# A planner that keeps accounts of every engine's queue, paired attention heads, and a reordered RWKV preparation in a hybrid encoder trunk

## The chip, the cores and the metric

The kernel runs on one core of one Trainium2 chip. The metric is the device time of one execution in microseconds (us), as the median of several runs.

## The reference

Two token groups, a prompt of 512 tokens and a sample of 256, pass through the same two layers with shared weights (model width 1024). A layer is a SwiGLU feed-forward half step, a mixer, and a second feed-forward half step, each behind an RMS norm that is scaled, shifted and gated by vectors made from a condition (`w_ada`). The mixer projects its input to 2432 columns (19 tiles of 128) and runs three head groups on them: a bidirectional gated linear recurrence (LRU), a bidirectional RWKV-7 with 4 heads of 64, and attention with 6 query heads on 2 key heads.

```python
def attention(q, k, v, q_g, k_g, rope):
    ...
        sc = jnp.einsum("bqkgd,bskd->bkgqs", qi, k) * scale
        p = jax.nn.softmax(sc, axis=-1)
        return jnp.einsum("bkgqs,bskd->bqkgd", p, v)
...
def layer(x, c, lp, rope):
    ...
    x = x + 0.5 * g1 * swiglu(h, lp["ffn_w_in"][0], lp["ffn_w_out"][0])
    h = rmsnorm(x, lp["norm_g"][1]) * (1 + sc2) + sh2
    x = x + g2 * mixer(h, lp, rope)
    h = rmsnorm(x, lp["norm_g"][2]) * (1 + sc3) + sh3
    x = x + 0.5 * g3 * swiglu(h, lp["ffn_w_in"][1], lp["ffn_w_out"][1])
```

## The kernel before

Activations lie transposed, 128 features on the partitions and the tokens along a row. The kernel calls the prompt `PS` (512 tokens, q.i = 0) and the sample `SS` (256 tokens, q.i = 1).

**Dense work.** Every product with a large weight (`mm3`) is made of three fp32r matmuls per 128x128 block: high part by high part, high by low, low by high. `wload` (lines 268 to 272) makes a weight's two parts: ScalarE copies the raw tile to `wh`, VectorE subtracts it to get `wl`, both inside `tc.high_priority(offset=60)`, which lets them stand up to 60 instructions ahead of their place in the program. Seven tiles of each part are held (`NW`). On TensorE the dense products go by the names of what they write: `pg`, `pu` (feed-forward input, prompt), `pb` (the same, sample), `mip` (mixer input), `ops` (output projections). A matmul of 512 columns is the prompt's, of 256 the sample's.

**Other work.** `adaps` makes the condition vectors, `ssp` the norms' sums. In `attention`, a unit is one head of one block of 128 queries: `S` (scores, a contraction of 64 rows), a softmax on VectorE and ScalarE, `ptp` (four or two transposes of the probabilities) and `avp` (values, 64 output rows). The two heads of a pair, hh = 0 and 1, lie on the lower and the upper 64 partitions. `gps` are the LRU's gates. In `rwkv_pair` (two heads at a time) a preparation makes decay (`up`, scanned into `cu`), rate (`ap`, `aa`), the normed key (`kkp`, `kb`) and the bonus (`bp`), and from them `AR`, `BK` and a copy `B`; then come `scps`, the block inverse (`yps` and `dps`, four levels), and a chain over the chunks of 64 tokens, `zps`, `saps`, `stps`, each waiting for the one before by way of VectorE or ScalarE; at the end `ywp`, a group norm and `yp`.

**What sets the order.** TensorE's order is written by the program itself (`tc.manual_schedule` for that engine); the other engines follow the program's order by priority, as a scheduler places it. The program's order comes from a planner (`Sched`): each sequence has a dense thread, and attention, LRU, RWKV and the condition vectors are threads beside them. Every matmul moves the planner's clock on by a cost; a thread that yields a number is ready that much later; a ready thread that isn't dense goes first. The numbers are fixed in a table `LAT`, one per kind of step and sequence:

```python
LAT = {'R0': (1.0, 4.4), 'ACC': (7.4, 2.8), ...
    def step(self, th):
        ...
        if callable(r):
            th.cond = r
        else:
            th.ready = self.t + r
```

Of the kernel before, what the change touches and what calls it, by code (L numbers as in the profile page):

```python
# [15 lines left out]
KD = 8  # L16
# [35 lines left out]
NR = 4  # L52

# [7 lines left out]
class Sched:  # L61
# [9 lines left out]
    def step(self, th):  # L71
        try:
            r = next(th.gen)
        except StopIteration:
            th.done = True
            self.threads.remove(th)
            return
        th.cond = None
        if callable(r):
            th.cond = r  # L80
        else:
            th.ready = self.t + r

    def run(self):
        while self.threads:
            act = [th for th in self.threads if th.cond is None or th.cond()]
            assert act, "stuck"
            now = [th for th in act if th.ready <= self.t + 1e-9]
            if not now:
                self.t = min(th.ready for th in act)  # L90
                continue
# [6 lines left out]
            else:  # L98
                self.step(dn[0])
                self.debt = max(0.0, self.debt - (self.t - t0))  # L100

# [10 lines left out]
def trunk_kernel(ctx, tc, xT, cT, wadh, wada, wfi, wfo, wmi, wmo, prm, gatew, loraw, cst, rope, scanm, outT, dbg=None):  # L112
    nc = tc.nc
    V, A, G, PE = nc.vector, nc.scalar, nc.gpsimd, nc.tensor
    sch = Sched(RATIO)

# [4 lines left out]
    sm = ctx.enter_context(tc.tile_pool(name="small", bufs=5))  # L121
# [8 lines left out]
    def dbank(n=512, name="db"):  # L130
        return psd.tile([128, n], F32, name=name, tag="d")

    def sbank(n=512, name="sb"):
        return pss.tile([128, n], F32, name=name, tag="m")
# [11 lines left out]

    def mm(out, lhsT, rhs, start=True, stop=True, cost=None):
        PE.matmul(out, lhsT, rhs, start=start, stop=stop, skip_group_check=True)  # L148
        k, m, n = lhsT.shape[0], lhsT.shape[-1], rhs.shape[-1]
        if cost is not None:  # L150
            sch.t += cost
        elif rhs.dtype == F32R:
            sch.t += (n / 2.4 if n >= 256 else 213) * 1e-3
        else:
            conc = 1.0
            if m <= 32:
                conc = 4.0
            elif m <= 64:
                conc = 2.0
            sch.t += max(4 * max(n, m) / 2.4 / conc, 33.0) * 1e-3  # L160

    def trp(out, src, idn, cost=0.11):
        PE.transpose(out, src, idn)
        sch.t += cost
# [47 lines left out]
    def ada_load(src):  # L212
        u = adap.tile([128, 1024], F32, name="adaw", tag="adaw")
        nc.sync.dma_start(out=u, in_=src)
# [22 lines left out]
    def ada(l, m, lat):  # L237
        ps = sbank(256, name="adaps")
        for k in range(KD):
            for j, u in enumerate(ada_load(wada[l * 9 + m, k])):  # L240
                mm(ps[32 * j:32 * j + 32, :], sc[:, k, :], u, start=(k == 0), stop=(k == KD - 1))
            if k % ADQ == ADQ - 1:
                yield lat
# [20 lines left out]
    def wtile(dt, name):  # L264
        return wsp.tile([128, 512], dt, name=name, tag=name)
# [30 lines left out]
    def weight_raw(u):  # L296
        raw = wsp.tile([128, 1024], F32, name="wr", tag="wr", bufs=NR)
        nc.sync.dma_start(out=raw[:, :u.shape[-1]], in_=u)
# [40 lines left out]
    def mm3(out, q, xs, every):  # L339
        nk = len(xs)  # L340
        for k, (xh, xl) in enumerate(xs):
            if k % 4 == 0:
                wh, wl = wget(q)
            c = (k % 4) * 128
            for i, (a, b) in enumerate(((wh, xh), (wh, xl), (wl, xh))):
                mm(out, a[:, c:c + 128], b, start=(k == 0 and i == 0), stop=(k == nk - 1 and i == 2))
            if k % every == every - 1:
                yield 0.0
# [36 lines left out]
    class Norm:  # L385
# [19 lines left out]
        def apply(self):  # L405
            q, l, i = self.q, self.l, self.i
            self.x = []
            for k in range(KD):
# [11 lines left out]
                yield LAT["CH"][q.i] if k < KD - 1 else LAT["NRM"][q.i]  # L420

        def finish(self):
            yield LAT["ACC"][self.q.i]
# [96 lines left out]
    def mix_in(q, l, xs, M):  # L520
# [3 lines left out]
        nc.sync.dma_start(out=rp, in_=rope[:, :, 0:n])  # L524
# [70 lines left out]
    def attention(q, l, M):  # L595
        n, nt = q.n, q.nt
        yield lambda: M.stage >= 1
        yield LAT["A0"][q.i]
# [22 lines left out]
        yield LAT["A1"][q.i]  # L621
        units = [(j, qt, hh) for j in range(3) for qt in range(nt) for hh in range(2)]
        st = {}

        def stA(u):
            j, qt, hh = units[u]
            b0, c0 = 64 * hh, qt * 128
            S = sbank(n, name="S")
            mm(S, M.qs[j][b0:b0 + 64, c0:c0 + 128], kr[b0:b0 + 64, :])
            mx = tn(1, name="mx")  # L630
            V.tensor_reduce(out=mx, in_=S, axis=AX.X, op=ALU.max)
            c = (j * nt + qt) * 2 + hh
            nb = tn(1, name="nb")
            V.scalar_tensor_tensor(out=nb, in0=mx, scalar=-1.0, in1=rq[:, c:c + 1], op0=ALU.mult, op1=ALU.mult)
            Pm = small(n, name="P")
            ssum = tn(1, name="ssum")
# [642 lines left out]
```

## Time and profile before

| | |
|---|---|
| runs | 3457.16, 3459.14, 3462.76 us; median 3459.14 |
| the profiled execution | 3462.16 us, span 3459.2 us |
| TensorE matmul busy | 3341.5 us, 97% of the span |
| VectorE, ScalarE, GpSimd busy | 58%, 42%, 15% |
| mean granted TensorE clock | 0.986 |

In the rows further down, a matmul's time is from its start to its modelled end, and matmuls overlap, so what one costs is the distance from its start to the next one's. One fp32 matmul stands as two records. The number in brackets is idle time of the engine before the row, and what ended it.

### The profile page before, as it was taken

To read this page: it belongs to the slowest core of one execution; us is meant where nothing else is said; L and a number is where in the kernel's file an instruction comes from. 1 tells how busy PE (TensorE), PEld (TensorE's weight loads), DVE (VectorE), ACT (ScalarE), POOL (GpSimd) and SP (SyncE) were. 2 spreads that over 40 slices of the span, in tenths; PEclk is the share of its full clock that TensorE was granted. 3 is DMA by queue.
4 is the path that set the end of the run, shared out by engine and by line. 5 is a ranking of instruction groups with operands and counts; after the bars stand their busy time and mean duration, and the time that the engine had idled before them with its cause. 6 is when DMAs were issued, how large, how long until landed. Compare 5 with 4: busy or idle time off the path is not lost. (4 is left out here: it accounts for less than half of the span.)

```text
span 3459.2 us, 69173 instructions
## 1 busy us (share of the span) xinstructions
PE 3341.5 (97%) x28052; PEld 2734.0 (79%) x28052; DVE 2003.2 (58%) x3973; ACT 1448.2 (42%) x2730; POOL 512.1 (15%) x659
## 2 busy tenths in 40 slices
PE   7999999999899899999999999999899999999999
PEld 5777776678877777888888876788789978778899
DVE  4433365775776745546333476667557776446466
ACT  3322243644346433434333346534345564334354
POOL 1100020212221211111000111212211111111010
PEclk9999999999999999999999999999899999999999
DMA  7666674133342222423332331233245533223455
GB/s 276 219 206 208 203 270 145 57 104 113 100 153 93 83 80 83 132 90 119 92 98 86 119 114 62 79 110 102 82 161 164 179 106 108 63 91 125 138 177 161
DMA packets 151630, 445.80 MB, mean 129 GB/s; under 512 B 16912, under 2 KB 20752, under 8 KB 151312
## 3 DMA queue, kind: packets, MB, share of 16 engines
q1 hardware_dynamic: 151312, 441.39, 40.2%
q8 instruction: 220, 3.60, 0.4%
q14 instruction: 98, 0.80, 0.1%
HBM read 427.17 MB, written 14.16 MB: 128 GB/s over the span
## 5 line engine op out<-in xcount | busy, mean ns | idle before, releaser
L270 ACT ACTIVATE wh<-wr 128x512 fp32r<-128x512 f32 (+1 forms) x1368 | 816.6, 602 | 1572.1 <-PE ops L148 485.5
L271 DVE TENSOR_TENSOR wl<-wr,wh 128x512 fp32r<-128x512 f32 (+1 forms) x1368 | 907.3, 668 | 800.4 <-ACT wh L270 769.8
L148 PE MATMUL ops<-an,wh 128*128 128x512 f32 (+1 forms) x2816 | 717.8, 345 | 19.3 <-ACT an L351 7.3
L148 PEld LDWEIGHTS ops<-an,wh 128*128 128x128 f32 x2816 | 480.1, 190 | 99.1 <-issue 13.5
L148 PE MATMUL pb<-xn,wh 128*128 128x256 f32 x2816 | 525.1, 287 | 0.5 <-issue 0.5
L148 PE MATMUL ops<-an,wl 128*128 128x512 f32 (+1 forms) x1408 | 477.2, 339 | 0.1
L148 PE MATMUL pg<-xn,wh 128*128 128x512 f32 x1408 | 449.5, 400 | 7.8 <-ACT xn L417 5.9
L148 PEld LDWEIGHTS pb<-xn,wh 128*128 128x128 f32 x2816 | 433.6, 189 | 19.2 <-issue 11.2
L148 PE MATMUL pu<-xn,wh 128*128 128x512 f32 x1408 | 447.4, 399 | 0.0
L352 POOL TENSOR_TENSOR an<-sg,an 128x512 fp32r<-128x512 f32 (+1 forms) x176 | 192.3, 1093 | 1674.0 <-ACT an L351 1613.0
L148 PE MATMUL pb<-xn,wl 128*128 128x256 f32 x1408 | 396.4, 282 | 4.8 <-DVE wl L271 3.8
L431 DVE SCALAR_TENSOR_TENSOR x<-ops,gat,x 128x256 f32<-128x256 f32 (+1 forms) x352 | 215.8, 614 | 196.0 <-PE ops L148 190.6
L148 PE MATMUL mip<-xn,wh 128*128 128x512 f32 (+1 forms) x1216 | 314.2, 348 | 9.3 <-DVE f L583 2.9
L148 PEld LDWEIGHTS pg<-xn,wh 128*128 128x128 f32 x1408 | 260.1, 188 | 75.6 <-ACT xn L417 6.5
L148 PEld LDWEIGHTS pu<-xn,wh 128*128 128x128 f32 x1408 | 260.1, 188 | 65.5 <-issue 6.6
L148 PEld LDWEIGHTS ops<-an,wl 128*128 128x128 f32 x1408 | 267.0, 190 | 31.6 <-DVE wl L271 0.3
L148 PE MATMUL pg<-xn,wl 128*128 128x512 f32 x704 | 277.4, 394 | 0.0
L148 PE MATMUL pu<-xn,wl 128*128 128x512 f32 x704 | 276.8, 393 | 0.0
L148 PEld LDWEIGHTS pb<-xn,wl 128*128 128x128 f32 x1408 | 265.9, 189 | 6.0 <-DVE wl L271 4.8
L148 PEld LDWEIGHTS mip<-xn,wh 128*128 128x128 f32 x1216 | 208.2, 192 | 48.9 <-issue 12.3
L148 PE MATMUL mip<-xn,wl 128*128 128x512 f32 (+1 forms) x608 | 207.2, 341 | 0.0
L148 PEld LDWEIGHTS pg<-xn,wl 128*128 128x128 f32 x704 | 132.9, 189 | 30.7
(257 smaller groups left out, 3738.5 us busy)
## 6 DMA issues: line engine op xcount, KB each, us to landing
wr<-in_wfi_dram SPq DMA_DIRECT2D x352, 512.0 KB, 3.6
adaw<-in_wada_dram SPq DMA_DIRECT2D x128, 512.0 KB, 4.4
wr<-in_wfo_dram SPq DMA_DIRECT2D x192, 256.0 KB, 2.7
wr<-in_wfo_dram SPq DMA_DIRECT2D x128, 320.0 KB, 2.9
wr<-in_wmi_dram SPq DMA_DIRECT2D x76, 512.0 KB, 3.6
wr<-in_wmo_dram SPq DMA_DIRECT2D x32, 512.0 KB, 3.5
adaw<-in_wadh_dram SPq DMA_DIRECT2D x32, 256.0 KB, 5.2
xsp<-x SPq DMA_DIRECT2D x8, 512.0 KB, 3.6
```

The source lines that it names most:

```text
L148: PE.matmul(out, lhsT, rhs, start=start, stop=stop, skip_group_check=True)
L270: A.activation(out=hi[:, :n], in_=raw, func=AF.Copy)
L271: V.tensor_tensor(out=lo[:, :n], in0=raw, in1=hi[:, :n].bitcast(F32), op=ALU.subtract)
L352: eng.tensor_tensor(out=lo, in0=src, in1=hi.bitcast(F32), op=ALU.subtract)
L431: V.scalar_tensor_tensor(out=q.x[m], in0=ps, scalar=gat[l][:, i, m, q.i:q.i + 1], in1=q.x[m], op0=ALU.mult, op1=ALU.add)
```

## The change

The planner's clock stays, but the fixed numbers go where a step's result is known. `Engine` wraps VectorE, ScalarE and GpSimd and enters each instruction in an account (`Model`): how long it takes, when its inputs are written, when its bank is free. A thread now yields `At(time)`, the time at which the account says that its data are there; a matmul whose data are late moves the planner's clock to that time; a thread that needs several PSUM banks asks for them (`mo.banks`). Matmul costs are raised a little, and a change between dense and other work costs 0.1. The pool `small` has 7 buffers in place of 5.

Attention takes both heads of a pair as one unit, in three steps (`scores`, `turn`, `values`), with the two heads' matmuls next to each other. RWKV's preparation makes key norm and bonus first, takes the rate and its product with the key into `BK` early, and ends with `AR`; one addition goes from GpSimd to VectorE. The group norm at the end of a pair (`tail`) is a thread of its own, so the second pair may begin before it. `wload` loses its precedence.

```diff
@@ class Sched
+        elif isinstance(r, At):
+            th.ready = r.t
+        elif r > 0 and self.mo.step_last > 0:
+            th.ready = self.mo.step_last + 0.05
...
+class Model:
...
+    def mm(self, out, ins, cost, old):
+        t = self.sch.t
+        need = max(self.ready(*ins), self.free.get(self.keys(out)[0][0], 0.0))
+        if need > t + 0.02:
...
+            t = need
+        dense = ins[1].dtype == F32R
+        if dense != self.dense:
+            t += SWITCH
...
     def wload(raw, n):
         hi, lo = wtile(F32R, "wh"), wtile(F32R, "wl")
-        with tc.high_priority(offset=60):
-            A.activation(out=hi[:, :n], in_=raw, func=AF.Copy)
-            V.tensor_tensor(out=lo[:, :n], in0=raw, in1=hi[:, :n].bitcast(F32), op=ALU.subtract)
+        A.activation(out=hi[:, :n], in_=raw, func=AF.Copy)
+        V.tensor_tensor(out=lo[:, :n], in0=raw, in1=hi[:, :n].bitcast(F32), op=ALU.subtract)
...
-        units = [(j, qt, hh) for j in range(3) for qt in range(nt) for hh in range(2)]
+        units = [(j, qt) for j in range(3) for qt in range(nt)]
...
+            for hh in range(2):
+                b0 = 64 * hh
+                mm(S[hh], M.qs[j][b0:b0 + 64, c0:c0 + 128], kr[b0:b0 + 64, :], cost=n * 1.25e-3)
...
             for kt in range(nt):
-                mm(o[b0:b0 + 64, :], vt[:, kt * 128 + b0:kt * 128 + b0 + 64], PT[:, kt * 128:kt * 128 + 128],
-                   start=(kt == 0), stop=(kt == nt - 1))
...
+                for hh in range(2):
+                    b0 = 64 * hh
+                    mm(o[b0:b0 + 64, :], vt[:, kt * 128 + b0:kt * 128 + b0 + 64], PT[hh][:, kt * 128:kt * 128 + 128],
+                       start=(kt == 0), stop=(kt == nt - 1))
...
             if u < nu:
-                stA(u)
+                yield from mo.banks(2)
+                scores(u)
+                yield At(mo.ready(*(list(st[u - 1]) if u else [kr])))
+            if 1 <= u <= nu:
+                yield from mo.banks(2)
+                turn(u - 1)
...
             if u >= 2:
-                stC(u - 2)
-            if 1 <= u <= nu:
-                stB(u - 1)
-            yield LAT["A2"][q.i]
+                values(u - 2)
+                yield 0.0
...
+        kp, bp = sbank(n, name="kkp"), sbank(n, name="bp")
+        mm(kp, blk, ksq)
+        mm(bp, blk, bon)
+        V.tensor_tensor(out=bon, in0=v, in1=bp, op=ALU.mult)
+        rB = bc_rsqrt(kp, n, None, None, clamp=1e-24)
...
-        G.tensor_scalar(cs_, cs_, 1.0, None, ALU.add)
+        V.tensor_scalar(cs_, cs_, 1.0, None, ALU.add)
...
+            V.tensor_scalar(BK[d][:, :, 64:128], c3(at_[:, d, :]), d_["kah"][:, hp:hp + 1], d_["ka1"][:, hp:hp + 1], ALU.mult, ALU.add)
+            G.tensor_tensor(out=BK[d][:, :, 64:128], in0=BK[d][:, :, 64:128], in1=c3(k), op=ALU.mult)
...
+        M.tails.append(sch.spawn(tail()))
```

The number of instructions on each engine is the same before and after (21,880 matmuls and transposes on TensorE), and so are their shapes, but for small ones in the softmax and in the preparation. The order moves everywhere. Three places follow, each first as before and then as now.

TensorE, the prompt's attention in layer 0 (`S` scores, `avp` values, `ptp` transposes, `mip` and `pb` dense work of the prompt and of the sample), before:

```order
L148 MATMUL S<-qr 128x512
L148 MATMUL avp<-PT,sqz 64x128 x4
L163 MATMUL ptp<-cs,P 128x128 x4
L148 MATMUL mip<-xn,wh 128x512 x2
L148 MATMUL mip<-xn,wl 128x512
L148 MATMUL mip<-xn,wh 128x512 x2
L148 MATMUL mip<-xn,wl 128x512
```

and now:

```order
L315 MATMUL S<-qr 128x512 x2
L315 MATMUL pb<-xn,wh 128x256 x2
L315 MATMUL pb<-xn,wl 128x256
L315 MATMUL pb<-xn,wh 128x256 x2
L315 MATMUL pb<-xn,wl 128x256
L332 MATMUL ptp<-cs,P 128x128 x8
L315 MATMUL pb<-xn,wh 128x256 x2
L315 MATMUL pb<-xn,wl 128x256
L315 MATMUL pb<-xn,wh 128x256 x2
L315 MATMUL pb<-xn,wl 128x256
L315 MATMUL avp<-P,sqz 64x128 x8
```

Two heads' scores, transposes and values now stand together, and each of the three is a visit of its own between dense matmuls.

VectorE, the end of the first RWKV preparation of the prompt (`rB` and `kb` end the key norm, `sg` and `x` belong to the sample's feed-forward), before:

```order
L378 STREAM_TRANSPOSE rB<-y 128x512
L431 SCALAR_TENSOR_TENSOR x_112<-ops,gat_134,x_112 128x256
L763 TENSOR_TENSOR kb<-kb,rB 128x512
L271 TENSOR_TENSOR wl<-wr,wh 128x512 x2
L781 SCALAR_TENSOR_TENSOR AR<-kb,Pt 128x512 x2
L271 TENSOR_TENSOR wl<-wr,wh 128x512 x2
L784 SCALAR_TENSOR_TENSOR csum<-aa,kb 128x1024
L271 TENSOR_TENSOR wl<-wr,wh 128x512 x2
L787 SCALAR_TENSOR_TENSOR BK<-csum,cu 128x8x64 x2
```

and now:

```order
L129 STREAM_TRANSPOSE rB<-y 128x512
L129 TENSOR_TENSOR kb<-kb,rB 128x512
L129 SCALAR_TENSOR_TENSOR sg<-sg,pb 128x256
L129 TENSOR_SCALAR csum<-csum 128x1024
L129 TENSOR_TENSOR sg<-sg,pb 128x256
L129 SCALAR_TENSOR_TENSOR cu<-smk,csum 128x512 x2
L129 TENSOR_SCALAR BK<-aa,kah_4005,ka_0_4003 128x8x64 x2
L129 TENSOR_TENSOR wl<-wr,wh 128x512 x3
L129 SCALAR_TENSOR_TENSOR sg<-sg,pb 128x256
L129 TENSOR_TENSOR wl<-wr,wh 128x512
L129 TENSOR_TENSOR sg<-sg,pb 128x256
L129 SCALAR_TENSOR_TENSOR csum<-aa,kb 128x1024
```

The key norm now stands ahead of the scans that give `cu`, and the weights' low parts (`wl`) still stand between the preparation's instructions.

TensorE, the chain over the chunks in layer 0 where dense work runs out (the prompt's second pair), before:

```order
L148 MATMUL stps<-SAV,BT 64x64 x4
L148 MATMUL zps<-S_10243,AR 64x64 x4
L148 MATMUL saps<-zt,Th 64x64 x4
L148 MATMUL stps<-SAV,BT 64x64 x4
L148 MATMUL zps<-S_10243,AR 64x64 x4
L148 MATMUL ssp<-acc,cs 128x256
L148 MATMUL saps<-zt,Th 64x64 x4
```

and now:

```order
L315 MATMUL zps<-S_10849,AR 64x64 x4
L315 MATMUL saps<-zt,Th 64x64 x4
L315 MATMUL stps<-SAV,BT 64x64 x4
L315 MATMUL zps<-S_10849,AR 64x64 x4
L315 MATMUL saps<-zt,Th 64x64 x4
L315 MATMUL gps<-xc,gw 64x256 x4
L315 MATMUL stps<-SAV,BT 64x64 x4
L315 MATMUL gps<-xc,gw 64x256 x4
L315 MATMUL zps<-S_10849,AR 64x64 x4
L315 MATMUL saps<-zt,Th 64x64 x4
L315 MATMUL stps<-SAV,BT 64x64 x4
L315 MATMUL zps<-S_10849,AR 64x64 x4
```

In both orders some steps of the chain have no dense matmul between them; the stretch is longer now.

## Rows read from the trace of the kernel before

**Rows 1.** The page, part 1: busy time, share of the span and instructions of TensorE

```profile
PE 3341.5 (97%) x28052; PEld 2734.0 (79%) x28052; DVE 2003.2 (58%) x3973; ACT 1448.2 (42%) x2730; POOL 512.1 (15%) x659
```

**Rows 2.** Stretches from us to us: PE, PEld, DVE, ACT, POOL busy; clock; DMA

```profile
486.00:1160.00 674.00, 629.32 (x6692) 502.49 (x6693) 457.20 (x945) 325.81 (x636) 129.41 (x182) 0.97 0.36 117
1160.00:1990.00 830.00, 825.86 (x5205) 668.42 (x5204) 400.25 (x749) 289.15 (x519) 106.58 (x110) 1.00 0.32 98
1990.00:2830.00 840.00, 797.31 (x7973) 681.37 (x7972) 573.11 (x1161) 415.68 (x801) 143.02 (x189) 0.98 0.38 118
2830.00:3459.00 629.00, 623.16 (x5088) 534.32 (x5086) 361.33 (x722) 264.25 (x508) 79.62 (x116) 1.00 0.40 121
```

**Rows 3.** Who waited for whom: total us, times, longest us

```profile
PE ssp L148 <- DMA adaw<-in_wadh_dram: 14.0, 1, 14.0
PE scps L148 <- DVE BK L793: 13.8, 3, 6.1
...
PE pg L148 <- ACT xn L417: 5.9, 2, 5.5
```

**Rows 4.** Timeline of TensorE, one attention unit of the prompt, layer 1

```profile
2108.84 0.63 PE L148 MATMUL mip<-xn,wh 128*128 128x512 f32 x2
2109.31 0.40 PE L148 MATMUL mip<-xn,wl 128*128 128x512 f32 x1
2109.64 1.12 PE L148 MATMUL S<-qr 64*128 64x512 f32 x2
2110.69 1.09 PE L148 MATMUL avp<-PT,sqz 128*64 128x128 f32 x8
2111.71 0.66 PE L163 MATMUL ptp<-cs,P 128*128 128x128 f32 x4
2112.12 0.72 PE L148 MATMUL mip<-xn,wh 128*128 128x512 f32 x2
```

**Rows 5.** Timeline of TensorE, one attention unit of the sample, layer 1

```profile
2849.63 0.70 PE L148 MATMUL S<-qr 64*128 64x256 f32 x2
2850.26 0.65 PE L148 MATMUL avp<-PT,sqz 128*64 128x128 f32 x4
2850.84 0.44 PE L163 MATMUL ptp<-cs,P 128*128 128x128 f32 x2
```

**Rows 6.** Timeline of TensorE, RWKV decay and rate, two row halves side by side

```profile
703.33 0.69 PE L148 MATMUL up<-f,lw 64*128 64x512 f32 x1
703.33 0.69 PE L148 MATMUL ap<-f,lw 64*128 64x512 f32 x1
...
704.29 1.02 PE L148 MATMUL up<-f,lw 64*128 64x512 f32 x2
705.24 0.51 PE L148 MATMUL pb<-xn,wh 128*128 128x256 f32 x2
```

**Rows 7.** Timeline of TensorE, RWKV output, two column halves in turn

```profile
838.41 2.08 PE L148 MATMUL ywp<-SAV,SC 128*64 128x64 f32 x64
840.42 0.51 PE L148 MATMUL pb<-xn,wh 128*128 128x256 f32 x2
```

**Rows 8.** Timeline of VectorE, the first RWKV preparation of the prompt

```profile
709.84 1.23 DVE L750 TENSOR_TENSOR_SCAN cu<-smk,csum 128x512 f32<-128x512 f32 x1 [4.75 <-POOL csum L748]
...
718.31 0.70 DVE L368 STREAM_TRANSPOSE tT<-kkp 128x512 f32<-128x512 f32 x1
...
725.59 0.69 DVE L763 TENSOR_TENSOR kb<-kb,rB 128x512 f32<-128x512 f32 x1
```

**Rows 9.** Timeline of TensorE, chunk chain without dense work between its steps

```profile
989.21 0.53 PE L148 MATMUL zps<-S,AR 64*64 64x64 f32 x8 [0.46 <-DVE S L976]
990.54 0.45 PE L148 MATMUL saps<-zt,Th 64*64 64x64 f32 x8 [0.80 <-DVE zt L953]
991.36 0.77 PE L148 MATMUL stps<-SAV,BT 128*64 128x64 f32 x8 [0.37 <-ACT SAV L959]
```

**Rows 10.** The page, part 5: the low half of a weight

```profile
L271 DVE TENSOR_TENSOR wl<-wr,wh 128x512 fp32r<-128x512 f32 (+1 forms) x1368 | 907.3, 668 | 800.4 <-ACT wh L270 769.8
```

More of the change, by code (lines that the diff above doesn't have):

```diff
@@ L52, with __init__ @@
 NR = 4
+SWITCH = 0.1
+DMAT = 3.4
+class At:
+    def __init__(self, t):
+        self.t = t
 class Thread:
@@ L100, in run, with __init__, __getattr__, place @@
                 self.debt = max(0.0, self.debt - (self.t - t0))
+class Engine:
+    def __init__(self, real, m, kind):
+        self.real, self.m, self.kind, self.iv = real, m, kind, []
+    def __getattr__(self, name):
+        call = getattr(self.real, name)
+        def run(*args, **kw):
+            r = call(*args, **kw)
+            aps = [a for a in args if hasattr(a, "dtype") and hasattr(a, "shape")]
+            outs = [kw[k] for k in ("out", "accum_out") if kw.get(k) is not None]
+            ins = [v for k, v in kw.items() if k not in ("out", "accum_out") and hasattr(v, "dtype") and hasattr(v, "shape")]
+            if "out" not in kw:
+                outs, aps = outs + aps[:1], aps[1:]
+            self.m.op(self, name, outs, ins + aps, kw)
+            return r
+        return run
+    def place(self, t0, dur):
+        iv = self.iv
+        k = len(iv)
+        while k > 0 and iv[k - 1][1] > t0:
+            k -= 1
+        s = t0
+        while k < len(iv) and iv[k][0] < s + dur:
+            s = max(s, iv[k][1])
+            k += 1
+        iv.insert(k, (s, s + dur))
+        if len(iv) > 400:
+            del iv[:200]
+        return s + dur
@@ L342, in mm3 @@
             if k % 4 == 0:
+                wfill(q, look(q) + 1)
+                yield At(mo.ready(*q.wq[0], *xs[k], *xs[min(k + 1, nk - 1)]) if k else
+                         max(mo.ready(*q.wq[0], *xs[0], *xs[min(1, nk - 1)]), mo.free.get(out.tensor.name if hasattr(out, "tensor") else out.name, 0.0)))
                 wh, wl = wget(q)
+            elif k % every == 0:
+                yield At(mo.ready(*xs[k], *xs[min(k + 1, nk - 1)]))
             c = (k % 4) * 128
@@ L658, in stC, with turn, values @@
+        def turn(u):
+            ptp = [sbank(n, name="ptp") for hh in range(2)]
+            for hh in range(2):
+                for kt in range(nt):
+                    trp(ptp[hh][:, kt * 128:kt * 128 + 128], st[u][hh][:, kt * 128:kt * 128 + 128], ident)
+                A.activation(out=st[u][hh], in_=ptp[hh], func=AF.Copy)
+        def values(u):
+            j, qt = units[u]
+            o = sbank(128, name="avp")
             PT = st.pop(u)
             for kt in range(nt):
-                mm(o[b0:b0 + 64, :], vt[:, kt * 128 + b0:kt * 128 + b0 + 64], PT[:, kt * 128:kt * 128 + 128],
-                   start=(kt == 0), stop=(kt == nt - 1))
@@ L822, in rwkv_pair @@
             for c0 in range(0, nch, 4):
+                yield from mo.banks(2)
                 pp = [sbank(512, name="scps") for h in range(2)]
@@ L842, in rwkv_pair @@
         for e in range(nbk):
+            yield from mo.banks(2)
             pp = [sbank(wb, name="btps") for h in range(2)]
```

326 lines of the change are left out of this document (200 added, 126 removed).

## The prediction

> **What bounds the kernel now.** I read the page's busy times first: TensorE is busy for 3341.5 of 3459.2 us, 97% [rows 1], with no other engine above 58%. So time comes off in two ways only: less work on TensorE, or less of its 117.7 us of idleness. Next, the busy time by stretches [rows 2]. The two stretches in which a sequence is in its mixer, 486 to 1160 us and 1990 to 2830 us, hold 44.7 and 42.7 us of that idleness, 87.4 together, at a granted clock of 0.97 and 0.98 of 2.4 GHz (a mean, with short times at 1.2); the feed-forward stretches after them hold 4.1 and 5.8 at 1.00. A further 14.0 us is the wait for the first condition weights, before the first matmul [rows 3], which the change leaves alone. The waits name what is in the 87.4: three waits of `scps` for `BK`, the end of an RWKV preparation, are 13.8 us, and the worst wait of a dense product for its norm 5.5 [rows 3]; the rest are small waits of the chains. The timeline of TensorE, read at an attention unit, shows what the other way can give.
>
> **Attention: work that goes.** A unit of the prompt costs from one start to the next 1.05 us for `S`, 1.02 for `avp`, 0.41 for `ptp` [rows 4]; a unit of the sample 0.63 and 0.58 for the first two [rows 5]. `S` uses 64 of the 128 rows of the array, `avp` 64 of its columns. What happens when two such matmuls on different halves follow each other, the trace shows elsewhere. `up` and `ap`, both 64 rows and 512 columns but on different halves of the rows, start at the same moment, and the pair takes 0.96 us (703.33 to 704.29), while the lone `up` behind it takes 0.95 (to 705.24) [rows 6]: the second of a pair is free. For column halves, `ywp` alternates them: 64 records of 64 columns take 2.01 us, 0.031 each [rows 7], or 0.063 for 128 columns, where `avp` pays 1.02 / 8 = 0.13 [rows 4].
>
> The counts: per layer the prompt has 12 pairs of units and the sample 6, so 24 and 12 in all.
> - `S`: one of two is free. 24 x 1.05 + 12 x 0.63 = 32.8 us.
> - `avp`: a pair of the prompt has 16 records, 16 x 0.063 = 1.0, and I put 0.1 on it for entering and leaving so short a run; 2 x 1.02 - 1.1 = 0.94 us saved, and for the sample 2 x 0.58 - 0.6 = 0.56. 24 x 0.94 + 12 x 0.56 = 29.3 us.
> - `ptp` uses the whole array: nothing.
> - Visits. The last dense matmul before `S` takes 0.33 us (2109.31 to 2109.64) where two before it took 0.47 [rows 4], so a boundary costs about 0.1. Three visits per pair take the place of two, but elsewhere the new order joins runs: counted over the whole program, boundaries between dense and other matmuls go from 935 to 957. 22 x 0.1 = 2 us lost.
>
> Together -60 us. TensorE has no cover, so all of it is on the path, unless the softmax is then late: `avp` now follows `ptp` after two small dense runs, some 1.4 us in the order shown, with two copies by ScalarE between. That is one of the small waits below. The bounds are 0 (nothing runs side by side) and -66 (no entry cost, no visits). I take -60, since the nearest rows have the same row and column halves and the same type.
>
> The Trainium skill ("TensorE: Matmul & The Clock Gate", in "Measured speedup vs the span model") gives a gain below the ideal for packed matmuls, 3.07-fold for four row tiles and 2.38-fold for three column tiles. By an estimate from that, some 1.55-fold for two, the two savings would be about 44 us in place of 62. Rows 6 show 0.96 against 0.95, so here the pair is all but ideal; I keep the rows' value.
>
> **Idle time: waits that go, and new ones.** The fixed table gave the first preparation of the prompt a length that was too short by the 6.1 us of its wait [rows 3]. On VectorE one sees why: the scan of `cu` waits 4.75 us for GpSimd's addition to `csum` (709.84), and then the key norm, from `tT` at 718.31 to `kb` at 725.59, takes 7.3 us, because small dependent steps alternate with other sequences' work [rows 8]. The change moves the norm before the scans and the addition to VectorE. Between `up` and `scps` it leaves 249 dense matmuls of the sample in the first pair, where there were 48 + 15 + 135 = 198, and 216 in the second, where there were 216. So the chain is some 11 us shorter (4.75 of the wait and most of 7.3), and its cover not shorter: the 13.8 us go, but for one place in layer 1, where the sample's dense work ends and only 96 matmuls are left (about 11 us at 0.118 each, half of the 0.235 that one of the prompt takes, 0.47 for two [rows 4]). There I put 5 us back. The dense threads too now wait by the account rather than by a fixed number.
>
> What the new order lays bare is the chain over the chunks. A step without dense work next to it idles 0.46, 0.80 and 0.37 us [rows 9], 0.54 on average. Before, one place had six such waits; now one has 12 and one seven, so 19 x 0.54 = 10 us against 3. At the second of them, the sample's first pair in layer 0, a group norm and the prompt's norm end with no dense work left: the like cost 5.5 us before [rows 3], and I count two, 11 us. A norm of the sample with no cover in layer 1 is a third, 5 us. So about 10 + 11 + 5 + 5 = 31 us of the 87 are there in the new order, and I put 15 on top for waits too small to be counted, since VectorE's and ScalarE's queues are only modelled. Idle falls from 87 to about 46: -41 us. The bounds are -70 (the account is right nearly everywhere) and +15 (the bare places cost twice my figure, and small waits stay as they are). The clock of 0.97 and 0.98 may rise with it; I put that at nothing, as far as the busy rows don't show it.
>
> **Weights without precedence.** In the mixer stretches 592 weight pairs are split, 0.67 us on VectorE each [rows 10]. Before, both halves could pass up to 60 instructions; now a `wl` may stand behind a softmax or a preparation. What is queued behind it is the dense matmul that needs it, and then all of TensorE. I cost it at 0: the seven buffers let a split start once the tile seven places back has been used, 7 x 12 matmuls of 0.118 us, or 9.9 us, before its own use, which hides several instructions of 0.7 to 1.2 us [rows 8] in front of it. The order shows `wl` still standing between the instructions of the preparation. The bounds are 0 and 592 x 0.67 = 397 us.
>
> **Other edits.** The seven `small` buffers only lift waits. `tail` as a thread lets the second pair's preparation start under the first's group norm: it is in the covers counted above. Longer modelled matmuls and boundaries change only the order.
>
> **Sum.** The profiled execution took 3462.2 us, 3.0 over its span, and lies 3.0 above the median. 3462.2 - 60 - 41 = 3361 on its scale, 3358 on the median's.
>
> **Rivals.**
> - A. Attention only: the new bare places and small waits give back what the better covers bring, idle time stays at 87. For it speak the 19 chain steps without cover and that this planner's durations are a fit; against it, that `scps`' three waits have more cover now. 3459 - 60 = 3399 us.
> - B. `S` gains nothing: each pair of scores needs two banks at once and waits for the second as long as the pairing saves, or the two halves hold each other up in a way that `up` and `ap` don't show. Attention gives 60 - 33 = 27 us: 3459 - 27 - 41 = 3391 us. For it: each row half of `S` reads its own 64 rows of the same tiles, in two passes; against it, rows 6 do the same. The Trainium skill's figures above would lie between, at 3358 + 18 = 3376.
> - C. Slower: `wl` is late. Its place is VectorE's queue in the mixer stretches, busy 457 of 674 and 573 of 840 us [rows 2]. If every weight pair waits behind 0.3 us more, 592 x 0.3 = 178 us are lost, and the kernel takes 3358 + 178 = 3536. It decides from 101 / 592 = 0.17 us per pair, or one pair in four late by one `wl`. For it: VectorE is TensorE's nearest neighbour in these stretches, and a queue can't be passed. Against it: the 9.9 us of room, and that waits for `wl` don't stand among the large ones.
> - D. No change: A, and on top about 60 us of late weights or late `P` copies. 3459 us.
>
> **Chances.** Forecast 0.60, A 0.18, B 0.08, C 0.09, D 0.05. Forecast, A and B are all faster; of D I count 0.02 as within 0.2% (7 us, about what a measurement of this kernel can tell from no change), 0.01 as slower and 0.02 as faster. So faster 0.88, same 0.02, slower 0.10. The range reaches from 3310 (-66 and the better part of -70, and a little clock) to 3415 (A with attention at -45), and leaves out C, D and the ends of the bounds, some 0.2.
>
> **What would show it.** `S` as two pairs of records with equal starts, about 1.05 us from the first to the next matmul for two heads, and `avp` x16 in about 1.1 us. TensorE's busy time near 3280 us. Idle in the mixer stretches near 46, no wait of `scps` for `BK` above a microsecond in layer 0, and the largest waits at the chain of layer 0 and at norms of both sequences. If C holds, `pb` or `ops` wait for `wl` in the list of waits, by tens of us. If B holds, the records of `S` follow each other by half a microsecond. The prediction is wrong if TensorE's busy time falls by less than 40 us, or if its idle time grows.

## The result, and the profile of the changed kernel

The changed kernel takes 3423.7 us (median; 3419.4 to 3428.8), the kernel before 3458.2: a ratio of 0.990, 95% interval 0.9885 to 0.9914. It is faster by 34.5 us, where 100 were forecast, and lies above the forecast's range. The profiled execution spans 3422.0 us, against 3459.2.

First part 1 of the page of the changed kernel, which answers to [rows 1]:

```profile
PE 3291.8 (96%) x28052; PEld 2714.2 (79%) x28052; DVE 1997.2 (58%) x3917; ACT 1437.7 (42%) x2730; POOL 514.6 (15%) x659
```

TensorE is busy for 49.7 us less. Its idle time, the span without this, grew from 117.7 to 130.2 us. Of the two sums of the forecast (-60 of matmul time, -41 of idleness), the first came for the most part and the second with the other sign.

The stretches, which answer to [rows 2] (columns: stretch, its length, busy time of PE, PEld, DVE, ACT, POOL with instructions, granted clock, DMA share, GB/s):

```profile
486.00:1160.00 674.00, 621.81 (x7512) 506.94 (x7511) 474.63 (x992) 333.89 (x663) 137.44 (x202) 0.96 0.36 116
1160.00:1990.00 830.00, 824.65 (x4517) 672.68 (x4518) 383.87 (x693) 285.96 (x512) 98.09 (x94) 0.99 0.33 100
1990.00:2830.00 840.00, 795.71 (x8096) 686.31 (x8095) 586.37 (x1166) 431.64 (x841) 150.04 (x202) 0.97 0.38 119
```

TensorE idles for 52.2 and 44.3 us in the two mixer stretches: 96.5, where 87.4 stood before and 46 were forecast. In both the clock is a hundredth lower. The boundary at 1160 us falls into the bare place shown below; 1.3 us of its longest wait lie behind it.

TensorE's rows for `S` and `avp` in the grouped view, shapes apart (count | busy us, mean ns of one | idle before, and its releasers), first of the kernel before and then of the changed one:

```profile
L148 PE MATMUL avp<-PT,sqz 128*64 128x128 f32 x480 | 67.8, 280 | 0.7 <-ACT PT L649 0.7
L148 PE MATMUL S<-qr 64*128 64x512 f32 x96 | 53.9, 641 | 2.3 <-DVE qr L613 2.3
L148 PE MATMUL S<-qr 64*128 64x256 f32 x48 | 16.7, 428 | 0.0
```

```profile
L315 PE MATMUL avp<-P,sqz 128*64 128x128 f32 x480 | 35.3, 285 | 2.9 <-ACT P L129 2.8
L315 PE MATMUL S<-qr 64*128 64x512 f32 x96 | 29.3, 641 | 0.9 <-ACT P L129 0.9
L315 PE MATMUL S<-qr 64*128 64x256 f32 x48 | 8.7, 424 | 0.1
```

One matmul takes as long as before, and the busy time of the group is all but halved: 53.9 to 29.3, 16.7 to 8.7 and 67.8 to 35.3 us. So the two heads run side by side. Summed from each start to the next, without idle time, `S` falls by 30.0 and `avp` by 30.5 us.

The waits, answering to [rows 3] (total us, times, longest us):

```profile
PE ssp L315 <- DVE acc L129: 23.6, 4, 14.3
PE ops L315 <- ACT an L129: 11.3, 5, 4.7
PE ops L315 <- DVE wl L129: 10.3, 5, 5.7
PE yp L315 <- DVE sh L129: 9.6, 3, 7.2
...
PE pb L315 <- ACT xn L129: 6.8, 1, 6.8
PE pb L315 <- DVE wl L129: 5.6, 3, 3.2
...
PE yp L315 <- DVE yy L129: 4.1, 2, 3.4
```

No wait of `scps` for `BK` is left, as forecast, only one of 1.1 us for another operand. In its place stand norms (`ssp`, and `pb` behind one), the group norm (`yp`) and weights (`wl`). The longest wait of `ssp`, 14.3, is the one before the first matmuls, as before.

The timeline of TensorE shows the costliest place, the end of the sample's first RWKV pair in layer 0 (start us, us, operation, count, and the idle time just before with its releaser; `...` stands for rows left out):

```profile
1136.94 0.40 PE L315 MATMUL ops<-xo,wl 128*128 128x512 f32 x1
1137.26 0.45 PE L315 MATMUL saps<-zt,Th 64*64 64x64 f32 x8
1138.08 0.87 PE L315 MATMUL stps<-SAV,BT 128*64 128x64 f32 x8 [0.37 <-ACT SAV L129]
1139.92 1.10 PE L315 MATMUL ssp<-acc,cs 128*128 128x512 f32 x2 [0.97 <-DVE acc L129]
...
1152.02 1.22 PE L315 MATMUL kkp<-ksq,cs 128*128 128x256 f32 x2 [1.92 <-ACT ksq L129]
...
1161.34 1.12 PE L315 MATMUL yp<-cs,yy 64*64 64x64 f32 x16 [7.25 <-DVE sh L129]
...
1165.54 1.22 PE L315 MATMUL pg<-xn,wh 128*128 128x512 f32 x2
1166.56 0.63 PE L315 MATMUL pg<-xn,wl 128*128 128x512 f32 x1
1166.98 1.05 PE L315 MATMUL pg<-xn,wh 128*128 128x512 f32 x2
```

At 1137 us the last matmul of the prompt's mixer output (`ops` of `xo`) is done, and the next dense ones, the prompt's feed-forward (`pg`), start at 1165. In between TensorE has only the two sequences' chains and norms. But the wait of 7.25 us before `yp` is not only a want of work: the first normalized tiles of the prompt, which `pg` reads, are written long before, as VectorE's timeline shows, and `pg` stands behind `yp` because the planner ordered it so.

```profile
1148.83 1.41 DVE L129 SCALAR_TENSOR_TENSOR xn<-nx,mod,xn 128x512 fp32r<-128x512 f32 x2
```

No run moves `pg` ahead, so what this order costs was not measured. The first three matmuls of `pg` take 1.44 us, from 1165.54 to 1166.98. At full clock two of their kind take 0.47 [rows 4], so three 0.70. The granted clock of a few windows says why:

```profile
1120.00:1135.00 15.00, 15.00 (x160) 11.53 (x159) 5.49 (x11) 6.69 (x16) 6.13 (x11) 1.00 0.15 48
1135.00:1170.00 35.00, 22.19 (x171) 15.36 (x170) 29.63 (x84) 12.74 (x25) 6.16 (x10) 0.66 0.05 16
1170.00:1200.00 30.00, 30.00 (x357) 23.37 (x357) 17.20 (x35) 11.62 (x20) 7.19 (x9) 1.00 0.25 73
...
2392.00:2412.00 20.00, 5.75 (x30) 4.32 (x30) 18.17 (x39) 8.02 (x15) 9.84 (x10) 0.64 0.26 84
```

Where TensorE has 22.19 us of work in 35, or 5.75 in 20, the mean clock is 0.66 and 0.64, so most of the stretch runs at 1.2 GHz; right before and behind the first of them it is 1.00. This bare place is paid twice, as idle time and in the matmuls behind it. Over the whole span the changed kernel has

```profile
core 0: 3422.0 us, clock 0.981
```

where the kernel before had 0.986. With two levels, one half of the other, the share of time at 1.2 GHz is twice what the mean lacks of 1: 0.038 x 3422 = 130 us, against 0.028 x 3459 = 97.

### The profile page after: what moved, and what is told of

It is laid out like the page before. It is cut to its first block, busy times and chain, and to the rows that moved or that the text cites. A ratio compares the mean times of both kernels' runs of the same rounds, so it can differ in the third digit from the quotient of the medians.

```text
span 3422.0 us, 69106 instructions
## 1 busy us (share of the span) xinstructions
PE 3291.8 (96%) x28052; PEld 2714.2 (79%) x28052; DVE 1997.2 (58%) x3917; ACT 1437.7 (42%) x2730; POOL 514.6 (15%) x659
```

## The experiments

Theory at the start: the pairing gave what it promised, and the loss lies in the planner's account. The rivals were late weights (W) and a pairing that pays for itself with waits of its own (P). In the first four expectations B is still the theory that the order lays chains and norms bare. After these runs it split in two: the account's times are too tight (T), or it spaces the prompt's RWKV steps too wide, so that no feed-forward work is left for the sample's (B). All runs in one table; idle is the span without TensorE's busy time, and the last column the start of the last `yp` of the prompt's mixer in layer 0.

| kernel | median us | ratio to before [95%] | span | PE busy | idle | last `yp` |
|---|---|---|---|---|---|---|
| before | 3458.2 | 1 | 3459.2 | 3341.5 | 117.7 | 1014.5 |
| changed | 3423.7 | 0.990 [0.9885, 0.9914] | 3422.0 | 3291.8 | 130.2 | 1065.7 |
| prec_back | 3424.9 | 0.9904 [0.989, 0.9919] | 3417.6 | 3287.8 | 129.8 | 1066.8 |
| pair_only | 3418.1 | 0.9886 [0.9872, 0.9899] | 3415.7 | 3289.0 | 126.7 | 992.0 |
| account_only | 3488.8 | 1.0091 [1.0077, 1.0105] | 3481.5 | 3347.5 | 134.0 | 1097.4 |
| pair_prep | 3404.4 | 0.9846 [0.9828, 0.9864] | 3400.1 | 3280.5 | 119.6 | 961.9 |
| account_or_step | 3419.7 | 0.9892 [0.9879, 0.9905] | 3413.5 | 3282.5 | 131.0 | 965.6 |
| account_and_step | 3438.9 | 0.9943 [0.9932, 0.9955] | 3426.9 | 3286.2 | 140.7 | 1078.4 |
| no_bank_gate | 3436.8 | 0.9941 [0.9929, 0.9953] | 3437.2 | 3287.1 | 150.1 | 1075.4 |
| pair_prep_lead | 3404.4 | 0.985 [0.9837, 0.9862] | 3404.4 | 3289.8 | 114.6 | 976.0 |
| or_step_prep | 3415.5 | 0.9882 [0.9866, 0.9898] | 3412.1 | 3285.9 | 126.2 | 963.2 |
| pair_prep_no_tail | 3398.9 | 0.9833 [0.9819, 0.9847] | 3396.1 | 3283.4 | 112.7 | 972.6 |
| pair_prep_qk_lead | 3401.1 | 0.9835 [0.982, 0.985] | 3398.8 | 3285.3 | 113.5 | 960.1 |
| after_no_tail | 3455.4 | 0.9988 [0.9979, 0.9997] | 3453.4 | 3294.7 | 158.7 | 1084.7 |
| rwkv_fixed | 3406.3 | 0.9849 [0.9836, 0.9863] | 3406.9 | 3285.0 | 121.9 | 969.8 |
| attn_lru_fixed | 3423.4 | 0.9888 [0.9873, 0.9903] | 3424.4 | 3290.7 | 133.7 | 1062.7 |
| norm_dense_fixed | 3470.3 | 1.0036 [1.0024, 1.0049] | 3466.1 | 3301.9 | 164.2 | 1088.1 |
| no_tail_qk_lead | 3405.1 | 0.9848 [0.9835, 0.9862] | 3400.4 | 3280.2 | 120.2 | 974.7 |

**1. The parts one by one.** Precedence back in the changed kernel; the pairing alone on the kernel before; the changed kernel with the heads one by one; and on the kernel before the pairing with the new preparation and the separate thread for the group norm, but fixed step times and precedence.

```diff
 prec_back, on the changed kernel:
+        with tc.high_priority(offset=60):
             A.activation(out=hi[:, :n], in_=raw, func=AF.Copy)
             V.tensor_tensor(out=lo[:, :n], in0=raw, in1=hi[:, :n].bitcast(F32), op=ALU.subtract)
 pair_only, on the kernel before (scores, turn, values and the 7 small buffers as in the change):
+                scores(u)
+                yield LAT["A2"][q.i]
...
+                turn(u - 1)
+                yield 0.5 * LAT["A2"][q.i]
 account_only, on the changed kernel: stA, stB, stC and their loop of the kernel before
 pair_prep, on pair_only: the change's order of rwkv_pair up to the chain, and
+        M.tails.append(sch.spawn(tail()))
```

> The changed kernel with the precedence of 60 instructions put back on the two halves of a weight, and nothing else; the order on TensorE is the same instruction for instruction, only ScalarE's and VectorE's orders differ. Theory W (late weights ate the expected gain): the 15.9 us in which the changed kernel's TensorE sits idle for wl go back to a few, the waits hidden in the matmuls' tails and the low clock behind them go too, and the time falls by 25 to 40 us, to 3385 to 3400. Theory B (the order itself lays chains and norms bare): at most the visible part goes, some of it only to the next wait, 3412 to 3424.

> The kernel before with the paired attention alone (scores, turn and values as steps of one, a half and a half of the old step time, seven small buffers): fixed step times, precedence and the old RWKV preparation stay. If pairing is worth what its matmuls lose (60 us) and the rest of the change gives nothing or less, this takes about 3398 us and beats the changed kernel by 25. If pairing brings waits of its own (P copies late, banks), 3410 to 3425. Theory W expects the former, theory B too; a theory P (pairing pays for itself with waits) the latter.

> The changed kernel with the old attention, one head at a time, in the old step form: the account, the new preparation and the missing precedence stay. If the parts add up, it is 60 us above the changed kernel, 3484, so slower than the kernel before by 25: the account and the missing precedence together would then cost time. Theory P expects less, 3450 to 3465.

> The kernel before with the paired attention, the new RWKV preparation and the group norm as a thread of its own; fixed step times and precedence stay. The three waits of scps for BK (13.8 us) should go and nothing else come: 3380 to 3390 us by theories W and B, so 35 to 45 us below the changed kernel. If the shorter lead that the fixed step times now leave (138 dense matmuls of the sample in place of 198) is too short, the waits stay and it takes 3395 to 3405.

W falls: with precedence back the time is the same, although TensorE's waits for `wl` fall from 15.9 us to 1.7. Others have grown by as much; these three were 1.5, 2.8 and nothing in the changed kernel:

```profile
PE ops L315 <- DVE x L129: 8.0, 6, 2.7
...
PE avp L315 <- ACT P L129: 5.2, 5, 2.3
...
PE pb L315 <- DVE x L129: 5.0, 1, 5.0
```

The pairing alone is worth 40 us on the kernel before, 20 less than W and B expected and within the range of P: its matmul time falls by 52.5, and its idle time grows by 9. Under the account it is worth 65 (3488.8 against 3423.7), more than P allows. So its price in waits depends on the order around it. The preparation and the thread bring 14 more; the 3404.4 lie in the second of the ranges expected for `pair_prep`, not in that of W and B. The account on top of them costs 19 (3423.7 against 3404.4, with the precedence gone as well). Without pairing the account, the preparation and the missing precedence together are slower than the kernel before by 30.

So the theory at the start explains less than a third of the miss. `pair_prep`, without the account, has the matmul time that was forecast (3280.5 us), but its idle time is 119.6, where the forecast comes to 117.7 - 41 = 77: 46 of the 66 us that are missing are missing there too.

**2. Too tight or too wide.** One line of the planner decides when a step that issued work is due: at the account's end of that work. `account_or_step` takes the earlier of this and the old fixed time, `account_and_step` the later.

```diff
         elif r > 0 and self.mo.step_last > 0:
-            th.ready = self.mo.step_last + 0.05
+            th.ready = min(self.mo.step_last + 0.05, self.t + r)
```

> The changed kernel, with one line of its planner altered: a side step that reported a time (it yielded a positive step time and issued work) is due at the earlier of the account's end of that work and the old fixed step time, instead of always at the account's end. Theory B (the account spaces the prompt's mixer steps wider than the fixed times did, the prompt's mixer of layer 0 ends some 100 us later, at 1065 us instead of 961 in pair_prep, and the feed-forward matmuls that would cover the sample's mixer and its norm are used up by then): the prompt's last output transposes of layer 0 come near 970 us again, the bare chain of the sample between 1130 and 1160 us and the bare norm near 2393 to 2409 us go (some 30 us of TensorE's idle time), some 10 us of waits before the score products come back as in pair_prep: 3385 to 3405 us. Theory T (the account's times are too tight, and many short waits at the visits make the idle time): earlier steps make more of them: 3425 to 3450 us.

> The changed kernel, with the same line altered the other way: a side step is due at the later of the account's end and the old fixed step time. Theory B: the prompt's mixer is no shorter, the sample's chain is spread out again, so that the bare places stay or grow in layer 0: 3415 to 3440 us. Theory T: every step has more time, the short waits of the delta and value products, of the turns and of the chain go (some 15 to 20 us of the idle time): 3395 to 3412 us.

T as the only cause falls with the second: more time makes the kernel 15 us slower. B has its mechanism, but not its size, with the first, which came out between the two ranges. The prompt's mixer ends at 965 us again, and the bare chain is gone; but the time falls by 4 us only, and the intervals of the ratios overlap; other waits stand in the list of `account_or_step`:

```profile
PE scps L315 <- DVE AR L129: 21.5, 4, 7.6
```

The account was right that this preparation is long, and TensorE waits for it when the step is shorter.

**3. Banks, and leads.** `no_bank_gate` drops the planner's admission by PSUM bank (`bank = 0.0`, and `banks` returns at once). `pair_prep_lead` raises one step of `pair_prep`; `or_step_prep` is `account_or_step` with the account's end kept for this step; `pair_prep_qk_lead` raises another.

```diff
 pair_prep_lead:
-'PREP': (5.0, 8.2)
+'PREP': (9.0, 8.2)
 or_step_prep:
+            th.ready = self.mo.step_last + 0.05 if r in LAT["PREP"] else min(self.mo.step_last + 0.05, self.t + r)
 pair_prep_qk_lead:
-'A0': (8.0, 12.0)
+'A0': (8.0, 16.0)
```

> The changed kernel, without its planner's admission by PSUM bank: a side thread is no longer held until the account has a bank free, and the loops that wait for two or three banks are gone; the account's step times stay. Theory B with the bank admission as what widens the prompt's steps: the mixer of layer 0 ends earlier by some tens of us, 3395 to 3412 us. Theory B with the step ends as what widens them: the prompt's mixer ends within 20 us of where it does in the changed kernel, and the time stays, 3415 to 3430 us.

> The kernel with fixed step times, paired attention and the new preparation (pair_prep, 3404.4 us), with the prompt's step from the preparation to the score products raised from 5.0 to 9.0 us. If the waits before the score products (9.1 us in two places of layer 1) are lead time that nothing else replaces: 3395 to 3398 us. If the lead only moves the wait, because the prompt's mixer then ends some 15 us later per layer and the norm behind it stands bare instead: 3402 to 3410 us.

> As account_or_step (3419.7 us), but the step from the preparation to the score products keeps the account's end. If the 21.5 us that TensorE waited before the score products there are lead time that only that step lacked: they fall below 6 us, and the time to 3398 to 3408 us. If a wait that goes only gives its time to the next place without feed-forward work, as in pair_prep_lead (scps waits gone, 3404.4 us as before): 3412 to 3425 us.

> pair_prep (3404.4 us) with the sample's first attention step (norm of q and k) raised from 12 to 16 us. If the 6.2 us wait before the sample's first scores and the 3.9 us before its gate products behind it (1063 and 1076 us) are lead time: 3394 to 3400 us. If they are only moved: 3401 to 3410 us.

The admission by bank is not what widens the steps: without it the prompt's mixer ends 10 us later, not earlier. And it earns its keep, for 13 us are lost, which puts `no_bank_gate` above both of its ranges. In `pair_prep` 9.1 us of waits of `scps` stand in the list, in `pair_prep_lead` only one above a microsecond (1.1), and the time is the same to 0.1 us. In `or_step_prep` the 21.5 us of `scps` are gone and the time falls by 4, again with overlapping intervals; the list's second place is now a weight:

```profile
PE ssp L315 <- DVE acc L129: 20.7, 3, 14.0
PE ops L315 <- DVE wl L129: 16.0, 7, 5.8
```

With `prec_back`, these are three times that a wait went from the list and the time hardly moved. For `pair_prep_qk_lead` (3.3 us less) the intervals overlap too.

**4. The thread for the group norm.** The same line put back in two kernels:

```diff
-        M.tails.append(sch.spawn(tail()))
+        yield from tail()
```

> pair_prep (3404.4 us) with the group norm and output of a RWKV pair in line again, before the next pair's preparation, so that only paired attention and the new preparation are left of the change. If the 14 us between pair_only (3418.1) and pair_prep come from the new order of the preparation: 3401 to 3408 us. If they come from the second pair's preparation starting beside the first one's group norm: 3413 to 3421 us.

> The changed kernel with the group norm and output of a RWKV pair in line again, ahead of the next pair's preparation (as in pair_prep_no_tail, which is 5.5 us under pair_prep). If the next pair's preparation, started beside the group norm, takes VectorE's time from it and lengthens the waits before the transposed outputs (13.7 us in the changed kernel, 3.6 before): 3412 to 3420 us. If the account gives the preparation its place anyway and the separate thread only hides the group norm: 3424 to 3435 us, with waits before the transposed outputs above 15 us.

With fixed steps the thread is worth nothing: 3398.9 without it against 3404.4 with it, the intervals of the ratios overlapping, and below both ranges that I had given. In the changed kernel it is worth 32 us. Without it the list of `after_no_tail` begins so:

```profile
PE yp L315 <- DVE yy L129: 32.6, 6, 12.6
PE ssp L315 <- DVE acc L129: 25.3, 3, 14.0
```

The direction is that of my second expectation; the time, 3455.4, lies 20 us above its range. That a group norm costs TensorE so much fits B, by which the feed-forward matmuls run out under the account; this run alone does not show it.

**5. Which of the account's due times.** The old fixed times put back in one set of threads each, and the two quickest versions put together.

```diff
 rwkv_fixed:
-        elif r > 0 and self.mo.step_last > 0:
-            th.ready = self.mo.step_last + 0.05
 attn_lru_fixed (likewise A1, A2 and L0):
-        yield At(mo.ready(*M.sq))
+        yield At(sch.t + LAT["A0"][q.i])
 norm_dense_fixed (likewise ACC and XO; the At of mm3 become yield 0.0):
-                yield At(mo.step_last - 1.6)
+                yield At(sch.t + (LAT["CH"][q.i] if k < KD - 1 else LAT["NRM"][q.i]))
 no_tail_qk_lead: pair_prep_no_tail with 'A0': (8.0, 16.0)
```

> The changed kernel with the old fixed times for the steps that yield a positive step time (the RWKV steps and one of the LRU); attention, norms and feed-forward products stay with the account. If the RWKV steps are what the account spaces too wide (theory B): the prompt's mixer of layer 0 ends near 965 us, the sample's chain has feed-forward work between its steps, and the time is 3398 to 3412 us. If the other sets cost as much: 3415 to 3425 us.

> The changed kernel with the old fixed times for the attention and LRU visits alone. Theory B with the RWKV steps as cause: the prompt's mixer still ends after 1040 us, 3416 to 3430 us. If the attention's visits by readiness cost the rest: 3402 to 3412 us.

> The changed kernel with the old fixed times for the norms' and output splits, and with feed-forward products that no longer wait in the planner for their weights and inputs. Theory B with the RWKV steps as cause: 3416 to 3430 us, with more of the waits at the feed-forward products and norms. If the feed-forward products' waits in the account cost the rest: 3402 to 3412 us.

> pair_prep without the separate thread for the group norm (3398.9 us) and with the sample's first attention step at 16 us in place of 12 (3401.1 us by itself, against 3404.4). If the two add: 3394 to 3397 us. If the wait only moves again: 3398 to 3403 us.

The RWKV steps it is: with fixed times for them alone 17 of the 19 us come back (3406.3). The attention's visits make no difference. Fixed times for norms and feed-forward products, put in together, cost 47 us, far above both ranges. But that is their price beside the account's RWKV steps, and no gain of the account as such: with RWKV on fixed times, the account for all the rest (`rwkv_fixed`, 3406.3) is no better than fixed times for everything (`pair_prep`, 3404.4). The three results can't be added up. The two quickest versions don't add either (3405.1, intervals overlapping); of the 3399 to 3405 us in which the versions of `pair_prep` lie I can explain no further difference.

What remains in `rwkv_fixed` is idle time all the same, 121.9 us, headed by `scps` waiting for `AR` (16.6 us in four places). The step of the sample's chain that stood bare above, in its timeline:

```profile
1275.92 0.45 PE L313 MATMUL stps<-SAV,BT 128*64 128x64 f32 x8
1276.30 0.74 PE L313 MATMUL pu<-xn,wh 128*128 128x512 f32 x2
1276.88 0.39 PE L313 MATMUL pu<-xn,wl 128*128 128x512 f32 x1
1277.11 0.62 PE L313 MATMUL pu<-xn,wh 128*128 128x512 f32 x2
1277.57 0.40 PE L313 MATMUL pu<-xn,wl 128*128 128x512 f32 x1
1277.89 0.45 PE L313 MATMUL zps<-S,AR 64*64 64x64 f32 x8
```

and the window of this chain, with its clock:

```profile
1260.00:1295.00 35.00, 35.00 (x319) 25.85 (x313) 14.49 (x37) 10.97 (x26) 5.03 (x6) 1.00 0.17 47
```

Six feed-forward matmuls stand between two steps; 35.00 us of 35 are busy, the clock is 1.00. The prompt's mixer, read at its last `yp` in the view of that tile up to 1130 us (duration in ns: least, median, most; first and last start), of `rwkv_fixed`:

```profile
L313 PE MATMUL yp<-cs,yy x64: 218/218/267, 830.4 to 969.8; 64*64 64x64 f32 x64
```

and of the changed kernel, up to 1160 us:

```profile
L315 PE MATMUL yp<-cs,yy x64: 218/218/267, 873.1 to 1065.7; 64*64 64x64 f32 x64
```

The sample's mixer input starts, in the view of `mip` from 800 to 1100 us, first in `rwkv_fixed` and then in the changed kernel, at

```profile
L313 PE MATMUL mip<-xn,wh x136: 274/281/583, 1048.9 to 1100.0; 128*128 128x256 f32 x136
L315 PE MATMUL mip<-xn,wh x304: 274/281/582, 942.9 to 1061.0; 128*128 128x256 f32 x152
```

So in the changed kernel the sample has used up its feed-forward and is in its own mixer while the prompt's mixer still runs, to 1065.7; in `rwkv_fixed` the prompt's has ended at 969.8 before the sample's begins, and the prompt's feed-forward is there to cover it. And the sample's own steps are hurried: from the key norm of its first pair to that of its second (`kkp`, from 1000 to 1300 us, in the same order) the account takes 85 us where the fixed times take 112.

```profile
L313 PE MATMUL kkp<-ksq,cs x4: 378/378/483, 1180.9 to 1293.0; 128*128 128x256 f32 x4
L315 PE MATMUL kkp<-ksq,cs x4: 634/634/796, 1067.2 to 1152.6; 128*128 128x256 f32 x4
```

The four kernels that differ only in that one line make a square. The account alone gives 3423.7, the earlier of both 3419.7, the later of both 3438.9, the fixed times alone 3406.3. The account's late ends (they spread the prompt's steps) cost 33 us where the fixed times hold otherwise (3438.9 against 3406.3), but beside its early ends only 4, which is not clear of noise (3423.7 against 3419.7). Its early ends (they hurry the sample) cost 13 us where the fixed times hold otherwise (3419.7 against 3406.3), and gain 15 beside the late ones (3423.7 against 3438.9). So B and T each have a part in these 17 us: for RWKV the account differs from the fixed times to both sides, one difference makes up for part of the other, and taking back either alone brings little or harm. Why its ends are late for the prompt was not tried. The code gives a candidate: a step counts as ended with the last instruction it issued on any engine, whether or not the next step reads it.

## Why the prediction was wrong

**Attention: right.** -30.0 for `S` and -30.5 for `avp`, forecast -32.8 and -29.3. The expected records are in the timeline of the changed kernel: both heads' scores in 1.06 us to the next start, and sixteen value products in 1.02.

```profile
2115.17 1.13 PE L315 MATMUL S<-qr 64*128 64x512 f32 x4
2116.23 0.73 PE L315 MATMUL mip<-xn,wh 128*128 128x512 f32 x2
...
2127.61 1.09 PE L315 MATMUL avp<-P,sqz 128*64 128x128 f32 x16
2128.63 0.73 PE L315 MATMUL mip<-xn,wh 128*128 128x512 f32 x2
...
2130.22 1.12 PE L315 MATMUL S<-qr 64*128 64x512 f32 x2
2131.78 1.12 PE L315 MATMUL S<-qr 64*128 64x512 f32 x2 [0.45 <-ACT P L129]
```

Of the 36 pairs of scores 33 run like the first of these. In the other three the two heads follow each other, in two of them as in the last two rows, where the second waits for ScalarE's `P`, by the code for a bank: what rival B described. They make up about the 2.8 us by which `S` fell short, so B was seen and was small, and falls.

The Trainium skill ("TensorE: Matmul & The Clock Gate", "Measured speedup vs the span model") would have given some 1.55-fold by an estimate from its figures; this trace has 70.6 / 38.0 = 1.86-fold for `S` and 67.8 / 35.3 = 1.92-fold for `avp`. Rows 6 and 7 were the better guide.

**Weights: right in the time.** Waits of 15.9 us for `wl` did come, but taking them away gives nothing back in the changed kernel (`prec_back`); rival C falls.

**Clock: the step "I put that at nothing" failed.** I had only asked whether it would rise. It fell: 130 us at 1.2 GHz against 97. Busy time outside `S` and `avp` rose by 60.5 - 49.7 = 10.8 us; 2 us of it I had put on the additional visits. If all 33 additional us at the lower level had been matmuls, these would have taken 16 longer, so the clock can carry the rest; no run shows that it carries all of it.

**Idle time: this step failed most.** Forecast 46 in the mixer stretches, as 31 for bare places that I named and 15 "on top for waits too small to be counted". Measured 96.5. The named places, from the timeline, came near their price but for one: the bare chain steps idle for 9.2 us (forecast 10). At the sample's first pair in layer 0 it is 7.25 for the group norm, 1.92 for the next pair's key norm and 0.97 for the prompt's sum of squares, 10.1 together (11). The sample's norm in layer 1 costs 7.34 + 6.84 = 14.2 (5), because I had counted the wait for the sum of squares or that for the first normalized tile, and not both. `scps` has 1.3 (5). That is 35 against 31.

What remains, 1.3 us of the group norm lying behind 1160 us, is 96.5 - 33.5 = 63, where I had written 15. Before the change the same remainder was 87.4 - 13.8 [rows 3] - 5.5 for a norm - 3 for six chain steps [rows 9] = 65. I let 50 of these 65 us vanish without a row that said so, on the argument that an account knows durations better than a table, and they did not go: in the two stretches about 26 us of idle time stand before the output projections (16 before the change), 13 before the block inverse (18). That was not the account's doing alone. In no run, with the account or without it, is the idle time of the span below 112.7 (`pair_prep_no_tail`), 5 us under the kernel before; the forecast needed 41. Waits that were taken away one at a time came back elsewhere; why the sum of the small ones stays where it is, the runs leave open.

**Which rival.** A, attention alone with idleness as before, 3399 us, was nearest in mechanism: what came is the attention's 60.5 us, less 10.8 of other busy time and 12.5 more of idleness. These three make up the 37.2 us between the two profiled spans by their definition, so that they meet it proves nothing more. Of my two conditions for being wrong, idle time that grows is the one that came true.

## What to carry to other kernels

Take the work that leaves the bounding engine from neighbouring rows; it came out here within a few us. Let waits vanish from a forecast only one by one, each with a row, and ask of each what stands next behind it. Removing a wait moves it if a later place has no cover: count the work that serves as cover across the whole stretch, since steps of one chain that are spread wider use up what the next chain needs. When a planner replaces tuned constants, test it set by set and in both directions, for two errors can cancel; and don't add up what the sets are worth, for each is measured beside the others.

## What the runs showed of the hardware that was not expected

A bare place cost twice. In the windows shown, a chain with 22.19 us of work in 35 went with a granted clock of 0.66, and the same kind of chain with feed-forward matmuls between its steps, 35.00 in 35, with 1.00. The first three feed-forward matmuls behind the bare one took 1.44 us in place of 0.70. So a wait like this has to be priced at more than its length. And two matmuls on different halves of the array overlapped almost wholly not just in [rows 6, 7], but for two passes of 64x512 float32 that read two halves of the same tensors (53.9 to 29.3 us, with three of 36 pairs not side by side).
